# Feed-forwards of an encoder block: a fourth pair by seven products, five sums by DMA, a new head and new ends

## The chip, the cores and the metric

One core of a Trainium2 chip runs one program. The metric is the device time of one execution in microseconds. The engines are TensorE (PE in the profile; PEld is its weight load), VectorE (DVE), ScalarE (ACT), GpSimd (POOL) and SyncE (SP). Transfers between the chip's DRAM and its on-chip memory are issued by SP, ACT or POOL and run on 16 DMA engines.

## The reference, cut to what matters

A layer over 256 tokens of 2048 features: a feed-forward, a mixer of two kinds, attention into 256 memory tokens, a second feed-forward, a last normalisation. All inputs are float32.

```python
def swiglu_ffn(h, w_in, w_out):
    gate, up = jnp.split(h @ w_in, 2, axis=-1)
    return (jax.nn.silu(gate) * up) @ w_out

h = rms_norm(x, ffn1_norm[l])                       # x: (1, 256, 2048)
x = x + 0.5 * swiglu_ffn(h, ffn1_w_in[l], ffn1_w_out[l])   # w_in: (2048, 11264), w_out: (5632, 2048)
...
h = rms_norm(x, ffn2_norm[l])
x = x + 0.5 * swiglu_ffn(h, ffn2_w_in[l], ffn2_w_out[l])
return rms_norm(x, final_norm)
```

## The kernel before, in words

**Two parts for each number.** A float32 operand is split into a high part (a cast to the matmul's float32r format, on ACT) and a low part (the difference, on DVE). A product is three matmuls: high by high, high by low, low by high. `weights` (L112, L113) does this for most matrices; the feed-forwards' input product has `parts` (L339, L340).

**The input product of a feed-forward** is the class `FeedForward`. The 11264 columns are 11 groups of 512 gate and 512 up columns; the 2048 features are 16 k-tiles of 128. A raw weight tile is 128x1024 (512 KB), gate beside up. Group 0 (in `run`) is done k-tile by k-tile while x arrives: `gained` scales x by the norm's gains and splits it, `by_two` does 12 matmuls for a k-tile (lines 288 to 291). Groups 1 to 10 (`group`) take two k-tiles and two token halves together, as 2x2 block products: a pair is done either by eight block products (`eight`, a "C" in the pattern, 24 matmuls) or, in Strassen's way, by seven (`seven`, an "S", 21 matmuls, L275 to L277). The seven need sums of weight blocks (DVE, L388, L389, L394, L401), which are split like weights, and sums of x blocks, made once by `sides`. The pattern of the eight pairs is `SCSCSCCC`. The eight PSUM banks hold b1 to b8; after the last pair by seven a copy and four additions (L439 to L443) take up b1, b5, b6, b7, and at the end of the group four additions (L452) take the others, then `give` makes silu(gate) * up.

**Sums by DMA.** For three k-tiles of a group (`SUMMED`, k = 2, 7, 13, all in pairs by eight) the low part isn't made by DVE: `summed` writes the negated rounded weights to the low part (ACT, L358), the rounded weights to the high part (ACT, L359), and a DMA from POOL's queue reads the raw weights again and adds them to the low part (L360). These tiles have buffers of their own, `hl_s`, and in the first feed-forward also half of `more`. The loads for them go through the same ring of raw tiles as the others.

**Buffers.** Raw tiles: four of the pool `wraw` and five parts of `spare`, in a ring. Split tiles: three of the pool `whl` ("hl"), two of `ring`, and in the first feed-forward one more in `more`, which takes the place of x (`x_given`); x is then read again from its input (L559). In the second feed-forward x stays on chip, so there are two ring tiles and one `hl_s`.

**Order.** Each engine works its instructions in order. The order is made by a scheduler that runs over the traced program with a cost model; `issue_after` puts instructions on an engine behind a given one.

**The head.** SP loads pieces of x transposed, the first parameters, and the raw weights, in that order. The squares of x for the first norm (`x_squares`, L524, L525) load x untransposed into raw tiles of `wraw` at k = 5, 7, 9, 11.

**The end.** The last output product is made for one token half after the other. For each half: the addition to x (`add_up`, L1015), its squares (L1019), and in `give` (L1025 to L1042) the sum over four parts, the root with one correcting step, the scaling and the stores.

## Time and profile before

| | |
|---|---|
| median of 3 runs | 2106.61 us (2106.22 to 2111.86) |
| the profiled execution | 2108.84 us, span 2107.0 us |
| TensorE | 2084.5 us busy, 9764 matmuls |
| VectorE, ScalarE | 1576.8 and 1161.6 us busy |
| DMA | 442.34 MB, 210 GB/s on the mean |
| group 0 to 10 of the first feed-forward | 7 to 474 us |
| the same of the second | about 1390 to 1850 us |

In the rows of the profile `out<-in` names the tiles, x the count, then come the busy time and the mean of one in ns, then the time for which the engine stood idle before them with the releaser. In the rows of stages the columns are the window, its length, the busy time and count of PE, PEld, DVE, ACT and POOL, the granted clock, the share of the 16 DMA engines and GB/s. In a timeline: start, duration, engine, line.

### The profile page before, as it was taken

How to read it: one execution, taken by the hardware profiler on the slowest of the kernel's cores; microseconds unless marked ns; L12 is line 12 of the kernel's file. 1: busy time of each engine (PE TensorE's matmuls, PEld its weight loads, DVE VectorE, ACT ScalarE, POOL GpSimd, SP SyncE). 2: the span in 40 equal slices, each digit the busy share in tenths (PEclk: the TensorE clock that was granted, in tenths of full speed). 3: DMA queues.
4: the chain of work that ended last, by engine and by line, in shares of the span. 5: the costliest groups of instructions: out<-in, count | busy, mean ns of one | idle time of the engine just before them, and what ended most of it. 6: DMA issues, size and time to landing. Idle time of an engine off the chain costs nothing.

```text
span 2107.0 us, 26590 instructions
## 1 busy us (share of the span) xinstructions
PE 2084.5 (99%) x9764; PEld 1738.5 (83%) x9764; DVE 1576.8 (75%) x2215; ACT 1161.6 (55%) x1450; POOL 67.7 (3%) x83
## 2 busy tenths in 40 slices
PE   8999999999999999999999999999999999999998
PEld 6888888888888888888888888888888888888886
DVE  6888888876655589889877665777888887787754
ACT  7666566645544454445665454556665666554443
POOL 0000000000000000000000000000000000000000
PEclk9999999999999999999999999999999999999999
DMA  9778777855666676666565543686787778556664
GB/s 360 230 227 257 229 238 245 263 167 169 216 198 188 206 236 200 190 176 185 176 201 185 186 154 111 206 281 191 231 259 247 232 229 250 178 160 202 197 192 149
DMA packets 122244, 442.34 MB, mean 210 GB/s; under 512 B 13697, under 2 KB 13825, under 8 KB 121729
## 3 DMA queue, kind: packets, MB, share of 16 engines
q1 hardware_dynamic: 113184, 407.35, 58.8%
q0 software_dynamic: 8640, 32.51, 8.5%
q8 instruction: 76, 1.25, 0.2%
q10 hardware_dynamic: 288, 0.79, 0.1%
q14 instruction: 56, 0.45, 0.1%
HBM read 438.49 MB, written 2.10 MB: 209 GB/s over the span
## 4 chain that ended last, share of the span: by engine, by line
PE 84%; issue 11%; DMA 2%; ACT 1%; POOL 1%; DVE 1%; SPq 0%; POOLq 0%; ACTq 0%
PE acc L172 12%; PE acc L173 12%; PE acc L171 12%; PE acc L125 9%; PE acc L289 7%; PE acc L288 7%; PE acc L291 7%; PE acc L126 4%; PE acc L277 2%; PE acc L276 2%; PE acc L275 2%; PE aux L263 1%; PE acc L1066 1%; PE acc L1065 1%; PE acc L1067 1%
## 5 line engine op out<-in xcount | busy, mean ns | idle before, releaser
L113 DVE TENSOR_TENSOR hl<-raw,hl 128x1024 fp32r<-128x1024 f32 (+1 forms) x402 | 488.6, 1216 | 282.5 <-ACT hl L112 281.1
L112 ACT CAST hl<-raw 128x1024 fp32r<-128x1024 f32 (+1 forms) x402 | 419.7, 1045 | 481.6 <-PE acc L173 289.3
L339 ACT CAST hl<-spare 128x1024 fp32r<-128x1024 f32 (+1 forms) x135 | 131.8, 993 | 95.5 <-DVE spare L389 38.5
L340 DVE TENSOR_TENSOR hl<-spare,hl 128x1024 fp32r<-128x1024 f32 (+1 forms) x135 | 154.4, 1150 | 35.8 <-ACT hl L339 34.2
L288 PE MATMUL acc<-hl,x_hl 128*128 128x512 f32 x408 | 144.2, 394 | 9.7 <-ACT hl L339 9.7
L289 PE MATMUL acc<-hl,x_hl 128*128 128x512 f32 x408 | 149.9, 395 | 0.0
L340 DVE TENSOR_TENSOR hl<-raw,hl 128x1024 fp32r<-128x1024 f32 (+1 forms) x101 | 113.9, 1131 | 45.9 <-ACT hl L339 44.3
L339 ACT CAST ring<-spare 128x1024 fp32r<-128x1024 f32 (+1 forms) x99 | 97.2, 988 | 68.9 <-DVE spare L389 26.9
L340 DVE TENSOR_TENSOR ring<-spare,ring 128x1024 fp32r<-128x1024 f32 (+1 forms) x99 | 112.9, 1145 | 19.9 <-ACT ring L339 18.8
L291 PE MATMUL acc<-hl,x_hl 128*128 128x512 f32 x408 | 127.5, 392 | 0.0
L339 ACT CAST hl<-raw 128x1024 fp32r<-128x1024 f32 (+1 forms) x101 | 97.7, 977 | 51.8 <-PE acc L291 16.1
L172 PE MATMUL acc<-hl,x_hl 128*128 128x512 f32 x256 | 100.5, 392 | 0.2 <-DVE hl L113 0.2
L172 PE MATMUL acc<-hl,m_hl 128*128 128x512 f32 x256 | 100.4, 392 | 0.0
L173 PE MATMUL acc<-hl,m_hl 128*128 128x512 f32 x256 | 100.2, 391 | 0.0
L173 PE MATMUL acc<-hl,x_hl 128*128 128x512 f32 x256 | 99.8, 390 | 0.0
L288 PEld LDWEIGHTS acc<-hl,x_hl 128*128 128x128 f32 x408 | 76.8, 189 | 25.9 <-ACT hl L339 10.1
L289 PE MATMUL acc<-ring,x_hl 128*128 128x512 f32 x248 | 93.1, 389 | 0.0
L288 PE MATMUL acc<-ring,x_hl 128*128 128x512 f32 x248 | 91.2, 390 | 0.0
L171 PE MATMUL acc<-hl,m_hl 128*128 128x512 f32 x256 | 91.2, 393 | 0.0
L289 PEld LDWEIGHTS acc<-hl,x_hl 128*128 128x128 f32 x408 | 77.2, 190 | 16.9 <-DVE hl L340 1.1
L291 PEld LDWEIGHTS acc<-hl,x_hl 128*128 128x128 f32 x408 | 77.5, 190 | 16.4
L125 PE MATMUL acc<-x_hl,hl 128*128 128x512 f32 x256 | 91.0, 398 | 0.0
(359 smaller groups left out, 5173.9 us busy)
## 6 DMA issues: line engine op xcount, KB each, us to landing
spare<-in_ffn_w_in SPq DMA_DIRECT2D x192, 512.0 KB, 6.4
raw<-in_ffn_w_out SPq DMA_DIRECT2D x176, 512.0 KB, 3.8
raw<-in_ffn_w_in SPq DMA_DIRECT2D x160, 512.0 KB, 6.3
hl_s<-in_ffn_w_in POOLq DMA_DIRECT2D x44, 512.0 KB, 7.3
raw<-in_w_mix_vg SPq DMA_DIRECT2D x32, 512.0 KB, 4.6
raw<-in_w_k SPq DMA_DIRECT2D x32, 512.0 KB, 4.0
raw<-in_w_v SPq DMA_DIRECT2D x32, 512.0 KB, 4.4
raw<-in_w_mix_out SPq DMA_DIRECT2D x32, 512.0 KB, 4.6
```

The costliest lines, as they stand in the source:

```text
L112: nc.scalar.copy(out=hl[:, 0, :size], in_=raw[:, :size])
L113: newest[0] = nc.vector.tensor_tensor(out=hl[:, 1, :size], in0=raw[:, :size], in1=hl[:, 0, :size].bitcast(F32), op=ALU.subtract)
L125: nc.tensor.matmul(acc, lhsT=w_hi, rhs=x_hl, start=first, stop=False, skip_group_check=True)
L126: nc.tensor.matmul(acc[:, 0], lhsT=w_lo, rhs=x_hl[:, 0], start=False, stop=last, skip_group_check=True)
L171: nc.tensor.matmul(acc[t], lhsT=x[:, 0, s], rhs=hi[:, k], start=k0 + k == 0, stop=False)
L172: nc.tensor.matmul(acc[t], lhsT=x[:, 0, s], rhs=lo[:, k], start=False, stop=False)
L173: nc.tensor.matmul(acc[t], lhsT=x[:, 1, s], rhs=hi[:, k], start=False, stop=k0 + k == nk - 1)
L288: nc.tensor.matmul(acc[t][g], lhsT=x[:, 0, s], rhs=hi[:, cols[g]], start=(t, g) in first, stop=False)
L289: nc.tensor.matmul(acc[t][g], lhsT=x[:, 0, s], rhs=lo[:, cols[g]], start=False, stop=False)
L291: nc.tensor.matmul(acc[t][g], lhsT=x[:, 1, s], rhs=hi[:, cols[g]], start=False, stop=last)
L339: nc.scalar.copy(out=hl[:, 0, :n], in_=raw[:, :n])
L340: newest[0] = nc.vector.tensor_tensor(out=hl[:, 1, :n], in0=raw[:, :n], in1=hl[:, 0, :n].bitcast(F32), op=ALU.subtract)
```

## The change

- Pattern `SCSCSCSC` in both feed-forwards: four of the eight pairs by seven products. `sides` makes a fourth set of x sums at k = 15 of group 0.
- Five k-tiles of a group (2, 6, 7, 11, 14) are summed by DMA. Their raw loads have one, later two, raw tiles of their own, taken from the ring, which goes from nine to eight, later seven.
- ACT's work for the next summed tile is put behind the cast of the k-tile that follows.
- The second feed-forward also gets the third ring tile and the second tile for sums: x is stored to DRAM behind the attention (`kept`, four stores) and read again after the last group (`x_back`).
- Head: the gains and the first k-tile of x come as one array by ACT's queue, the first weight tile in two halves; 11 plain float32 matmuls of `ones` stand ahead of the first product (`WARM`); the squares of x use tiles of `h` and come at k = 2, 4, 6, 8; the other parameters come at k = 6.
- Group 0's `give` stands ahead of `x_given` and of the second `summed`.
- In the last group two instead of four of the transposes that follow are done beside the last pairs.
- The end: three of the four sums of squares are added ahead of the last part; the fourth is added as the bias of the root; one operation changes its form.

```diff
-PATTERNS = ("SCSCSCCC", "SCSCSCCC")
-SUMMED = ((2, 7, 13), (2, 7, 13))
+PATTERNS = ("SCSCSCSC", "SCSCSCSC")
+SUMMED = ((2, 6, 7, 11, 14), (2, 6, 7, 11, 14))
+WARM = 11
...
+    gx = xt.tile([P, KD + KD * T], F32, name="gx", tag="x")
+    gains, xT = gx[:, :KD], gx[:, KD:].rearrange("p (k t) -> p k t", t=T)
+    nc.scalar.dma_start(out=gx[:, :KD + T], in_=a["gains_x0"])
+    nc.scalar.dma_start(out=xT[:, 1], in_=a["xT"][:, 1])
+    nc.vector.memset(ones, 1.0)
+    idle = pa.tile([P, 2, T], F32, name="aux")
+    for _ in range(WARM):
+        nc.tensor.matmul(idle[:, 0, :P], lhsT=ones, rhs=ones, start=True, stop=True)
...
+    def x_given():
+        more = xt.tile([P, 4, 1024], F32R, name="more", tag="x")
+        ff.ring.append(more[:, :2])
+        ff.hls.append(more[:, 2:])
+        ff.raws_summed.append(ff.raws.pop())
+    def x_back(src):
+        xT = xt.tile([P, KD, T], F32, name="xT", tag="x")
+        for k in range(0, KD, 8):
+            nc.gpsimd.dma_start(out=xT[:, k:k + 8], in_=src[:, k:k + 8])
+        return xT
...
     (FeedForward.__init__)
+            self.raws_summed = [self.raws.pop()]
     (summed)
-            raw, hl = self.raw(j, k), self.hls[at % len(self.hls)]
+            raw, hl = self.raws_summed[at % len(self.hls)], self.hls[at % len(self.hls)]
+            nc.sync.dma_start(out=raw, in_=self.w_in[j, :, k])
     (end of seven)
+            if self.next is not None:
+                with tc.issue_after(self.cast.ins):
+                    self.summed(self.next)
+                self.next = None
     (eight)
-                if at is not False:
-                    self.summed(at + len(self.hls))
+                if self.next is not None:
+                    with tc.issue_after(self.cast.ins):
+                        self.summed(self.next)
+                self.next = None if at is False else at + len(self.hls)
     (group)
-                    if p > self.spairs[-1] + 1:
+                    if p >= n - 2:
...
+        def early(self, before):
+            self.raw_at += 1
+            self.at += 1
+            raw = wraw.tile([P, 1024], F32, name="raw")
+            hl = whl.tile([P, 2, 1024], F32R, name="hl")
+            halves = [slice(G, 2 * G), slice(0, G)]
+            for s in halves:
+                nc.sync.dma_start(out=raw[:, s], in_=self.w_in[0, :, 0, s])
+            x = before(0)
+            for s in halves:
+                with tc.issue_after(x.ins):
+                    split(hl[:, 0, s], hl[:, 1, s], raw[:, s])
+            return hl
     (run)
+            self.give(0, [acc[t][0] for t in range(2)], [acc[t][1] for t in range(2)], r)
             if more is not None:
                 more()
                 self.summed(1)
-            self.give(0, [acc[t][0] for t in range(2)], [acc[t][1] for t in range(2)], r)
...
-                    now, turns = turns[:4], turns[4:]
+                    at = 2 * self.pattern[-2:].count("C")
+                    now, turns = turns[:at], turns[at:]
...
     (x_squares)
-        raw = wraw.tile([P, 1024], F32, name="raw")
+        raw = ff.h[7 - c].rearrange("p a b -> p (a b)")
     (x_arrives)
-            if k % 2 == 0:
+            if k > 0 and k % 2 == 0:
                 nc.sync.dma_start(out=xT[:, k:k + 2], in_=a["xT"][:, k:k + 2])
-            if k == 0:
-                nc.sync.dma_start(out=pv[:, :head], in_=a["pv"][:, :head])
     (x_more)
-            if k in (5, 7, 9, 11):
-                x_squares(k // 2 - 2)
-            if k in (6, 9, 12):
+            if k in (2, 4, 6, 8):
+                x_squares(k // 2 - 1)
+            if k in (6, 9, 12, 15):
                 ff.sides(k // 3 - 2)
...
     (the output product of the attention)
+                if f % 4 == 3:
+                    nc.gpsimd.dma_start(out=kept[:, f - 3:f + 1], in_=xT[:, f - 3:f + 1])
...
-        turns = ff.run(lambda k: None, first_beside, lambda: rms_cols(ss, D, "r_x2"))
+        turns = ff.run(lambda k: None, first_beside, lambda: rms_cols(ss, D, "r_x2"), x_given)
+        xT = x_back(kept)
...
     (the end)
-            nc.vector.reduce_sum(out=tot, in_=sums[:, t], axis=AX.X)
-            nc.scalar.activation(out=s, in_=tot, func=AF.Sqrt, scale=1.0 / D, bias=eps)
-            nc.vector.tensor_scalar(out=v, in0=tot, scalar1=1.0 / D, scalar2=RMS_EPS, op0=ALU.mult, op1=ALU.add)
+            last = sums[:, t, 3:4]
+            nc.scalar.activation(out=s, in_=last, func=AF.Sqrt, scale=1.0 / D, bias=most[t])
+            nc.vector.tensor_scalar(out=v, in0=last, scalar1=1.0 / D, scalar2=most[t], op0=ALU.mult, op1=ALU.add)
             nc.vector.reciprocal(out=r, in_=s)
-            nc.vector.scalar_tensor_tensor(out=r, in0=v, scalar=r, in1=s, op0=ALU.mult, op1=ALU.add)
+            nc.vector.tensor_scalar(out=r, in0=v, scalar1=r, scalar2=s, op0=ALU.mult, op1=ALU.add)
```

More of the change, by code (lines that the diff above doesn't have):

```diff
@@ L237, in gained @@
     def gained(dst, k, x, g):
-        nc.scalar.activation(out=dst[:, k, 0], in_=x, func=AF.Copy, scale=g)
+        part = nc.scalar.activation(out=dst[:, k, 0], in_=x, func=AF.Copy, scale=g)
         nc.vector.scalar_tensor_tensor(
@@ L242, in gained @@
         )
+        return part
     def gained_tile(tag):
@@ L338, in parts @@
             hl = whl.tile([P, 2, 1024], F32R, name="hl") if last or i < 3 else self.ring[i - 3]
-            nc.scalar.copy(out=hl[:, 0, :n], in_=raw[:, :n])
+            self.cast = nc.scalar.copy(out=hl[:, 0, :n], in_=raw[:, :n])
             newest[0] = nc.vector.tensor_tensor(
@@ L367, in sides @@
             for q in range(2):
-                nc.scalar.activation(out=xg[:, q], in_=xT[:, k + q], func=AF.Copy, scale=col(self.gain, k + q))
+                nc.scalar.activation(out=xg[:, q], in_=xT[:, k + q], func=AF.Copy, scale=self.gain(k + q))
             a11, a21, a12, a22 = xg[:, 0, :P], xg[:, 0, P:], xg[:, 1, :P], xg[:, 1, P:]
@@ L453, in group, with run @@
             self.give(j, (p1, u2), (u4, u5), r)
-        def run(self, before, after, root, more=None):
+        def early(self, before):
[11 more added lines that the diff above has]
+            return hl
+        def run(self, before, after, root, more=None, early=False):
             acc = token_accs()
@@ L459, in run @@
             for k in range(KD):
-                before(k)
-                w = self.parts(self.raw(0, k))
+                if k == 0 and early:
+                    w = self.early(before)
+                else:
+                    before(k)
+                    w = self.parts(self.raw(0, k))
                 begin = [(t, g) for t in range(2) for g in range(2)] if k == 0 else []
@@ L548, in x_root @@
             return r_x
-        def x_given():
-            more = xt.tile([P, 4, 1024], F32R, name="more", tag="x")
-            ff.ring.append(more[:, :2])
-            ff.hls.append(more[:, 2:])
-        turns = ff.run(x_arrives, x_more, x_root, x_given)
-        xT = xt.tile([P, KD, T], F32, name="xT", tag="x")
-        for k in range(0, KD, 8):
-            nc.gpsimd.dma_start(out=xT[:, k:k + 8], in_=a["xT"][:, k:k + 8])
+        turns = ff.run(x_arrives, x_more, x_root, x_given, early=True)
+        xT = x_back(a["xT"])
         sm = st.tile([P, T], F32, name="sm")
@@ L1022, in give @@
         def give(t, parts):
[L1024 to L1027 removed]
+            v, s, r = [st.tile([P, 1], F32, name=f"{n}{t}") for n in ("f_v", "f_s", "f_r")]
+            last = sums[:, t, 3:4]
+            nc.scalar.activation(out=s, in_=last, func=AF.Sqrt, scale=1.0 / D, bias=most[t])
+            nc.vector.tensor_scalar(out=v, in0=last, scalar1=1.0 / D, scalar2=most[t], op0=ALU.mult, op1=ALU.add)
             nc.vector.reciprocal(out=r, in_=s)
[L1029 removed]
+            nc.vector.tensor_scalar(out=r, in0=v, scalar1=r, scalar2=s, op0=ALU.mult, op1=ALU.add)
             nc.vector.reciprocal(out=r, in_=r)
@@ L1050, in layer @@
         finish()
+        st.tile([P, 8], F32, name="to_64_too")
+        most = [st.tile([P, 1], F32, name=f"f_most{t}") for t in range(2)]
+        for t in range(2):
+            nc.vector.reduce_sum(out=most[t], in_=sums[:, t, 0:3], axis=AX.X)
+            nc.vector.tensor_scalar(
+                out=most[t], in0=most[t], scalar1=1.0 / D, scalar2=RMS_EPS, op0=ALU.mult, op1=ALU.add
+            )
         warm = nc.scalar.activation(out=st.tile([P, 1], F32, name="warm"), in_=ones[:, 0:1], func=AF.Sqrt)
```

25 lines of the change are left out of this document (11 added, 14 removed).

## The prediction

> **What bounds the kernel now.** I read the page first (busy time, slices, DMA queues), then the busy time by stage, then the order of time inside a feed-forward group. From the page:
>
> ```profile
> span 2107.0 us, 26590 instructions
> ...
> PE 2084.5 (99%) x9764; PEld 1738.5 (83%) x9764; DVE 1576.8 (75%) x2215; ACT 1161.6 (55%) x1450; POOL 67.7 (3%) x83
> ...
> q1 hardware_dynamic: 113184, 407.35, 58.8%
> q0 software_dynamic: 8640, 32.51, 8.5%
> ```
>
> TensorE is busy 99% of the span. A busy TensorE can still wait inside its pipeline, so the next question is the spacing of the starts. Two rows of the timeline of TensorE within a group of the first feed-forward; the first and the last of 49 consecutive starts, with 48 matmuls of 128x512 from one to the other:
>
> ```profile
> 329.66 0.39 PE L275 MATMUL acc<-ring,x_hl 128*128 128x512 f32 x1
> ...
> 340.54 0.39 PE L288 MATMUL acc<-hl_s,x_hl 128*128 128x512 f32 x1
> ```
>
> 10.88 / 48 = 0.2267 us for one matmul, without a gap. The stages (columns: length, then busy time and count of PE, PEld, DVE, ACT, POOL, then granted clock, DMA share, GB/s):
>
> ```profile
> 0.00:7.10 7.10, 0.00 (x0) 0.00 (x0) 2.15 (x9) 4.68 (x10) 0.70 (x6) 1.00 0.72 220
> 7.10:41.85 34.75, 34.74 (x143) 28.36 (x144) 25.77 (x39) 29.02 (x44) 1.88 (x2) 1.00 1.03 386
> 41.85:58.00 16.15, 13.57 (x53) 10.44 (x52) 8.46 (x15) 8.54 (x10) 0.00 (x0) 0.89 0.80 289
> 58.00:473.50 415.50, 415.03 (x1836) 343.25 (x1835) 339.99 (x406) 250.34 (x278) 24.62 (x29) 1.00 0.74 233
> ...
> 1435.00:1850.00 415.00, 414.03 (x1830) 341.99 (x1829) 335.64 (x403) 251.18 (x275) 24.38 (x28) 1.00 0.76 230
> ...
> 2097.00:2107.00 10.00, 0.03 (x1) 0.00 (x0) 4.02 (x11) 3.29 (x7) 1.26 (x1) 0.67 0.55 211
> ```
>
> 1830 matmuls at 0.2267 are 414.9 us: the ten groups of the second feed-forward (415.00) are nothing but matmuls, and those of the first (415.5) nearly so. A matmul left out there is worth its 0.2267 us, as long as the other engines and the DMA keep up. Beside this stand three places where TensorE does not run: 7.1 us at the start, the head (143 matmuls take 34.75 us where 32.4 would do; 53 take 16.15 where 12.0 would do), and 10 us at the end.
>
> **The change, part by part.**
>
> *Matmuls.* A pair by seven products is 7 x 3 = 21 matmuls, by eight 24. One more pair by seven in each of ten groups of both feed-forwards: 20 x 3 = 60 matmuls fewer, 60 x 0.2267 = 13.6 us. Group 0 keeps its 192.
>
> *DVE and ACT per group.* Their prices, by form, from the steady part of the first feed-forward:
>
> ```profile
> L340 DVE TENSOR_TENSOR hl<-spare,hl 128x1024 fp32r<-128x1024 f32 x38 | 46.1, 1221 | 6.0 <-ACT hl L339 5.7
> ...
> L388 DVE TENSOR_TENSOR spare<-raw 128x512 f32<-128x512 f32 x12 | 8.2, 687 | 5.2 <-DMA raw<-in_ffn_w_in 5.2
> ...
> L340 DVE TENSOR_TENSOR hl<-raw,hl 128x512 fp32r<-128x512 f32 x7 | 4.8, 690 | 3.4 <-ACT hl L339 3.1
> ...
> L339 ACT CAST hl<-spare 128x1024 fp32r<-128x1024 f32 x39 | 40.5, 1050 | 27.2 <-DVE spare L389 18.5 <-PE acc L277 4.1 <-DMA spare<-in_ffn_w_in 2.7
> ...
> L339 ACT CAST hl<-raw 128x512 fp32r<-128x512 f32 x7 | 4.3, 619 | 5.1 <-DVE raw L401 5.1
> ```
>
> and the same stretch and one of the second feed-forward as a whole (eight and seven groups):
>
> ```profile
> 100.00:432.00 332.00, 332.00 (x1466) 274.99 (x1466) 275.17 (x329) 203.56 (x226) 20.90 (x24) 1.00 0.77 242
> 1518.00:1808.00 290.00, 289.28 (x1276) 239.27 (x1275) 239.37 (x287) 179.63 (x196) 18.33 (x21) 1.00 0.79 240
> ```
>
> A seven costs DVE four half operations (0.69), three whole ones (1.22) and a half one (0.69): 7.1 us; a k-tile in the plain way 1.22. Of the k-tiles in eights, 7 were plain; now 3 of 8 are (five are summed by DMA). So DVE changes by +7.1 - 4 x 1.22 = +2.2 us: from 275.17/8 = 34.4 to 36.6 us, in a group that shrinks from 41.5 to 40.8 us: 83% to 90%. ACT: +3.8 (three casts of 1.05 and one of 0.62) - 4 x 1.05 + 2 summed tiles at two operations of about 1.05 = +3.8: 25.4 to 29.2 us, 72%. Both stay under the matmuls; this I cost at nothing where work is spread, and what covers it is the lead of three tiles "hl" and now three of the ring in both feed-forwards. The lead is real now: ACT waited for TensorE (rows below).
>
> *DMA.* Each summed tile is read twice. From the queue rows an accumulating transfer (0.524 MB; 62 of them in q0's 32.51 MB) takes 8.5% x 2107 / 62 = 2.9 us of all 16 engines. Two more per group: the share goes from 0.77 x 41.5 = 32.0 to 37.8 of 40.8 us, 0.92 (second feed-forward 0.94), at (16 + 5) x 0.524 MB / 40.8 us = 270 GB/s. The head sustained a share of 1.03 and 386 GB/s while TensorE ran, so the transfers fit; they land later. Seven raw tiles for 11 loads that remain in the ring, beside two of the summed tiles' own, replace nine for 16: 26 us of holding time against 23, so I cost the smaller ring at nothing.
>
> *The summed chain.* After TensorE's last reading of a summed tile come ACT's negated copy, POOL's issue, the landing, and TensorE's next use. One such chain of the second feed-forward, from k=2 to k=7, and the landings of all:
>
> ```profile
> 1687.11 0.61 PE L291 MATMUL acc<-hl_s,x_hl 128*128 128x512 f32 x2
> ...
> 1687.31 1.07 ACT L358 ACTIVATE hl_s<-spare 128x1024 fp32r<-128x1024 f32 x1 [1.17 <-PE acc L289]
> ...
> 1688.78 0.87 POOL L360 DMA_DIRECT2D hl_s<-in_ffn_w_in  x1 [12.04 <-ACT hl_s L358]
> ...
> 1698.22 0.39 PE L288 MATMUL acc<-hl_s,x_hl 128*128 128x512 f32 x1
> ```
>
> ```profile
> DMA to landing us min/median/max: 5.3/7.3/9.8
> ```
>
> The chain is 1.67 us and a landing; 11.1 us are there (45 matmuls and the end of a tile). With two tiles a summed k-tile uses the buffer of the one two before it: 2 to 7 and 6 to 11 have this distance, 7 to 14, 11 to the next 2 and 14 to the next 6 have 15 us or more. So 40 tight chains in all, with a margin of 2.1 us at the median landing, none at 9.4. In the old first feed-forward every distance was longer, in the second one two of three were as tight, and cost
>
> ```profile
> PE acc L289 <- DMA hl_s<-in_ffn_w_in: 1.0, 2, 0.7
> ```
>
> 1.0 us in all at a DMA share of 0.79. Bounds for the new one: 0 (none late) and 40 x 0.8 = 32 us (each landing as late as 9.8 or a little more, where the scheduler leaves less than 11.1). I take 2.5 us, near the measured 1.0, for twice the tight chains of which some land later. The new place of the casts changes the order on ACT: the copy now stands behind the next k-tile's cast, which runs ahead of TensorE, so it is not held up; nothing is gained on the path either. At group ends the last seven is now followed by one pair of eight (5.4 us) instead of three (16.3): four DVE additions and a copy, some 3.4 us, must free the banks in it. They fit; I add 1 us in all for this and for bursts (0 to 8 by 20 ends at 0.4).
>
> *Head.* Rows of the first 45 us:
>
> ```profile
> 0.84 0.17 DVE L186 MEMSET ones<- 128x128 f32 x1 [0.84 <-PEq L1135]
> ...
> 7.11 2.07 PE L288 MATMUL acc<-hl,x_hl 128*128 128x512 f32 x4 [7.11 <-ACT hl L339]
> ...
> 42.69 1.06 ACT L525 ACTIVATE raw<-raw 128x1024 f32<-128x1024 f32 x1 [1.92 <-DMA raw<-in_x]
> ```
>
> ```profile
> 874.72 0.60 PE L774 MATMUL aux<-wT,vs 128*128 128x128 f32 x4
> ```
>
> The first matmuls come 0.43 us apart (four in 2.07 us), twice the later spacing. The filler is 11 matmuls of plain f32; the last row is two such (four passes, about 0.11 each at the full clock), so one costs 0.22, or 0.44 at the slow start: 11 x 0.44 = 4.8 us from about 1.1, to 5.9 us. The data are there by then: smaller loads, with no wait for the parameters. So the real start moves from 7.1 to 5.9 (-1.2), and of the 2.3 us lost to slow matmuls I take 1.6 back (bounds 0 and 2.3). The 4.1 us lost after 41.85 began with ACT waiting for a late piece of x (row L525), which had waited for a raw tile; x's squares now have tiles of their own and come three k-tiles sooner, so this wait goes. What is late next is the weights: the DMA was full from 7 to 42 us (1.03), the bytes are the same and TensorE comes 3 us sooner. I take half: -2.1 (bounds 0 and -4.1).
>
> The Trainium skill (TensorE: Matmul & The Clock Gate, section "What's actually happening") has a free-running window of 3413 ns after which the clock is released; the slow start here is in keeping with it. By that rule a filler begun at 1.1 us releases the clock between about 4.5 and 7.9 us, and this term would lie between -2.3 and -1.3, so the sum would move by less than a microsecond.
>
> *Ends.* Rows of the first token half's end:
>
> ```profile
> 2095.60 0.16 DVE L1025 TENSOR_REDUCE f_tot<-sums 128x1 f32<-128x4 f32 x1 [0.79 <-ACT sq L1019]
> 2095.64 1.30 POOL L1020 TENSOR_TENSOR spare<-spare,gf 128x512 f32<-128x512 f32 x1 [53.70 <-ACT sq L1019]
> 2095.79 0.15 DVE L1027 TENSOR_SCALAR f_v<-f_tot 128x1 f32<-128x1 f32 x1
> ...
> 2096.32 0.64 DVE L1029 SCALAR_TENSOR_TENSOR f_r<-f_v,f_r,f_s 128x1 f32<-128x1 f32 x1
> ```
>
> The reduction leaves the chain (0.19) and the form of 0.64 becomes one of 0.15: -0.68 in each half. The first half's chain keeps DVE from the second's addition, so both count: -1.3 us.
>
> *x in DRAM.* Four stores of 512 KB and a load of 2 MB, on POOL's queue, under matmuls; the load is wanted about 3 us after the last group and can start when the third ring tile is done, before the last pair. Nothing, at worst 4 us once. Two transposes fewer ahead of the output product: the same.
>
> **Sum.** -13.6 - 1.2 - 1.6 - 2.1 - 1.3 + 2.5 + 1.0 = -16.3 us. The profiled execution took 2108.84 us (span 2107.0), so it would take 2092.5; the median of the three runs stands 2.2 us below it, and so my time is 2090 us.
>
> **The rivals.**
>
> *A. Late accumulates (slower).* If the landing under a share of 0.92 to 0.94 passes 9.4 us as a rule, TensorE waits twice a group. At 0.8 us it is 32 us instead of 2.5: 2090 + 29.5 = 2120. It outweighs the gains of 19.8 us from 0.5 us a chain. For it: landings up to 9.8 already. Against it: at 0.79 TensorE lost only the 1.0 us above, and the head moved 386 GB/s. The Trainium skill (SBUF — State Buffer, "Who interferes with whom" and the warning above it) says that descriptors for POOL's transfers wait while DVE holds a shared port, which would feed this rival; it also says that an addition with two SBUF inputs blocks only reads, and that fits POOL's even 0.87 us here.
>
> *B. DVE and ACT become the bound.* These rows of the waits, over all 20 groups:
>
> ```profile
> DVE hl L340 <- ACT hl L339: 78.5, 76, 5.1
> ...
> DVE ring L340 <- ACT ring L339: 33.3, 38, 2.9
> ...
> ACT hl_s L358 <- PE acc L289: 31.8, 30, 3.7
> ...
> ACT hl L339 <- PE acc L291: 25.6, 23, 1.9
> ```
>
> DVE waits 112/20 = 5.6 us a group for casts. Were this forced by the order (sum, cast, difference), DVE would need 36.6 + 5.6 = 42.2 us against 40.8, 1.4 x 20 = 28 us, 2118; with half of it forced, 39.4, no loss. In between, 41.7 gives +18, 2108: no change. Against: ACT itself waits for TensorE, so much of the idle time is lead.
>
> *C. The head stays as it was.* The DMA is full there whatever is asked for: without -4.9 us, 2095.
>
> *D. Everything goes well.* No stall, the whole head: -13.6 - 1.2 - 2.3 - 4.1 - 1.3 = -22.5: 2084.
>
> **Chances.** My case with C and D as its edges (2083 to 2098): 0.70. A mild form of A or B with still a gain (2098 to 2100): 0.07; about no change (2100 to 2113): 0.09; clearly slower: 0.14. What a measurement can tell from no change is some 0.3%, 6.3 us. So faster 0.77, same 0.09, slower 0.14. The range reaches from 2082 to 2106, the likeliest case's own from 2083 to 2098.
>
> **What would show it.** Right: 22 records of filler and 60 matmuls fewer than before, groups of 40.8 us with DVE at 0.90 and the DMA share at 0.92; first matmul on weights near 5.9 us and no gap near 42; waits of TensorE for the two summed tiles of a few microseconds in all; no 0.6 us operation in the end. Wrong: groups over 41.2 us; TensorE waiting for L340 or L339 (B) or for the accumulates (A); ACT or DVE waiting for raw tiles for more than now. The prediction fails if landings grow beyond 9.4 us, or if the tight chain starts later on ACT than 0.2 us after TensorE's last reading.

## The result and the profile after

| | median | range |
|---|---|---|
| before | 2106.61 us | 2106.0 to 2111.86, 5 runs |
| after | 2128.6 us | 2125.21 to 2132.5, 5 runs |

The ratio is 1.0101 (95% interval 1.0089 to 1.0112): the change made the kernel 1% slower. The prediction was 2090.

The page of the kernel after (span, busy times, and POOL's DMA queue with the accumulating transfers):

```profile
span 2123.4 us, 26702 instructions
...
PE 2093.7 (99%) x9726; PEld 1730.7 (82%) x9726; DVE 1614.3 (76%) x2307; ACT 1221.7 (58%) x1537; POOL 104.7 (5%) x129
...
q0 software_dynamic: 15264, 57.68, 13.9%
```

TensorE has fewer matmuls (9726 records for 9764: 60 fewer, and 22 of the filler) and is busy 9 us longer. A busy share of 99% says nothing here; the stages do. First before, cut at starts of matmuls (start, group 0, groups 1 to 10, the stretch from the first output product on, and so on; the groups end with the start of their last matmul; columns as in the prediction):

```profile
0.00:7.11 7.11, 0.00 (x1) 0.00 (x1) 2.16 (x9) 4.69 (x10) 0.70 (x6) 1.00 0.72 220
7.11:57.53 50.42, 47.84 (x193) 38.40 (x193) 33.74 (x53) 37.08 (x54) 1.88 (x2) 0.97 0.96 358
57.53:474.48 416.95, 416.48 (x1843) 344.42 (x1842) 341.44 (x408) 250.81 (x278) 24.62 (x29) 1.00 0.74 233
474.48:1386.46 911.98, 910.57 (x4562) 769.21 (x4561) 659.72 (x1038) 475.65 (x668) 1.18 (x9) 1.00 0.61 187
...
1430.46:1847.75 417.29, 416.32 (x1838) 343.91 (x1837) 337.48 (x403) 253.27 (x278) 24.38 (x28) 1.00 0.76 230
1847.75:2096.64 248.89, 248.89 (x1137) 206.07 (x1136) 165.30 (x249) 109.47 (x125) 12.53 (x7) 1.00 0.61 180
2096.64:2107.00 10.36, 0.39 (x2) 0.00 (x0) 4.35 (x12) 3.29 (x7) 1.56 (x2) 0.68 0.53 203
```

The same stages after:

```profile
0.00:5.77 5.77, 4.71 (x23) 4.71 (x23) 1.06 (x3) 3.15 (x8) 0.70 (x6) 1.00 0.68 225
5.77:50.96 45.19, 44.51 (x194) 36.23 (x194) 37.66 (x66) 38.63 (x60) 1.03 (x1) 1.00 1.03 392
50.96:472.69 421.73, 414.80 (x1801) 336.35 (x1800) 355.01 (x443) 281.79 (x317) 42.92 (x50) 1.00 0.86 254
472.69:1393.43 920.74, 917.35 (x4575) 771.67 (x4573) 662.67 (x1041) 476.91 (x671) 2.78 (x12) 1.00 0.61 188
...
1437.41:1854.84 417.43, 413.34 (x1800) 336.62 (x1799) 354.94 (x442) 279.97 (x314) 41.98 (x49) 1.00 0.86 254
1854.84:2113.88 259.04, 254.66 (x1146) 208.58 (x1144) 168.05 (x258) 108.53 (x128) 11.53 (x7) 0.99 0.59 178
2113.88:2123.40 9.52, 0.39 (x2) 0.00 (x0) 3.53 (x9) 3.20 (x7) 1.48 (x2) 0.78 0.57 221
```

The head gained 6.6 us (1.34 and 5.23), the end 0.84. The groups should have gained 13.6 us and lost instead: +4.8 in the first feed-forward and +0.1 in the second. And two stages that the prediction left alone lost 18.9: the stretch that begins with the first output product +8.8, the second output product +10.2. Together this is +16.4 us, the difference of the spans.

What makes these up is read from the starts of consecutive matmuls of 128x512. What a step has above 0.2267 us is an excess; in a step under 0.30 us it is counted as slow spacing, in a longer one as a wait or as a matmul at half the clock (0.43 us):

| us against before | matmuls | waits and half clock | slow spacing | transposes moved out of the groups, and other shapes |
|---|---|---|---|---|
| groups, both feed-forwards | -13.6 | +13.7 | +6.6 | -1.8 |
| after them, both output products | 0 | +9.6 | +5.1 | +4.1 |

The 4.1 us hold the two waits for ACT of 0.8 us each that stand behind transposes. TensorE's waits after (what was waited for: us in all, times, longest):

```profile
PE acc L303 <- DMA more<-in_ffn_w_in: 7.5, 9, 2.0
PE acc L176 <- DVE hl_s L124: 5.2, 2, 3.6
PE acc L289 <- DVE spare L489: 1.9, 4, 0.8
PE acc L174 <- ACT hl_s L123: 1.6, 2, 0.8
...
PE aux L289 <- DVE spare L479: 0.8, 1, 0.8
PE acc L303 <- DMA hl_s<-in_ffn_w_in: 0.7, 1, 0.7
```

So there are three suspects: the groups, with tiles summed by DMA that come late (first and last row) and waits for DVE's evictions (third and fifth); the start of the output products (second and fourth); and a spacing of matmuls that no wait explains. Each was taken apart on the chip. The kernel before was timed again beside each set of runs (medians 2107.1 to 2108.6 us); the ratios below are taken against those runs.

### The profile page after: what moved, and what is told of

The parts are those of the page before. It is cut to its first block, busy times and chain, and to the rows that moved or that the text cites. A ratio compares the mean times of both kernels' runs of the same rounds, so it can differ in the third digit from the quotient of the medians.

```text
span 2123.4 us, 26702 instructions
## 1 busy us (share of the span) xinstructions
PE 2093.7 (99%) x9726; PEld 1730.7 (82%) x9726; DVE 1614.3 (76%) x2307; ACT 1221.7 (58%) x1537; POOL 104.7 (5%) x129
## 3 DMA queue, kind: packets, MB, share of 16 engines
q10 hardware_dynamic: 576, 1.06, 0.1%
## 4 chain that ended last, share of the span: by engine, by line
PE 67%; issue 26%; DMA 3%; POOL 3%; ACT 1%; DVE 1%; SPq 0%; POOLq 0%; DVEq 0%; ACTq 0%
PE acc L176 12%; PE acc L175 12%; PE acc L174 12%; PE acc L128 8%; PE acc L129 4%; PE acc L303 3%; PE acc L305 2%; PE acc L302 2%; DMA more<-in_ffn_w_in 2%; POOL hl_s L391 1%; POOL more L391 1%; PE aux L277 1%; PE acc L291 1%; PE acc L290 1%; PE acc L289 1%
## 5 line engine op out<-in xcount | busy, mean ns | idle before, releaser
L116 DVE TENSOR_TENSOR hl<-raw,hl 128x1024 fp32r<-128x1024 f32 (+1 forms) x402 | 488.7, 1217 | 290.4 <-ACT hl L115 289.4
L370 DVE TENSOR_TENSOR hl<-spare,hl 128x1024 fp32r<-128x1024 f32 (+1 forms) x102 | 116.7, 1146 | 12.0 <-ACT hl L369 11.7
L369 ACT CAST hl<-spare 128x1024 fp32r<-128x1024 f32 (+1 forms) x102 | 100.1, 989 | 38.2 <-DVE spare L432 16.0
L369 ACT CAST hl<-raw 128x1024 fp32r<-128x1024 f32 (+1 forms) x109 | 101.8, 944 | 33.7 <-DVE raw L432 25.2
L369 ACT CAST ring<-spare 128x1024 fp32r<-128x1024 f32 (+1 forms) x84 | 82.2, 988 | 54.4 <-PE acc L291 27.4
L370 DVE TENSOR_TENSOR ring<-spare,ring 128x1024 fp32r<-128x1024 f32 (+1 forms) x84 | 95.4, 1143 | 19.0 <-ACT ring L369 18.7
L175 PE MATMUL acc<-hl,x_hl 128*128 128x512 f32 x256 | 100.5, 393 | 0.0
L176 PE MATMUL acc<-hl,x_hl 128*128 128x512 f32 x256 | 99.9, 390 | 0.0
L303 PE MATMUL acc<-more,x_hl 128*128 128x512 f32 x240 | 89.2, 394 | 7.5 <-DMA more<-in_ffn_w_in 7.5
L128 PE MATMUL acc<-o_hl,hl 128*128 128x512 f32 x256 | 90.6, 399 | 0.0
L128 PE MATMUL acc<-y_hl,hl 128*128 128x512 f32 x256 | 90.5, 399 | 0.0
L174 PE MATMUL acc<-hl,x_hl 128*128 128x512 f32 x256 | 90.0, 391 | 0.0
L175 PE MATMUL acc<-hl,hA 128*128 128x512 f32 x224 | 87.9, 392 | 0.0
L175 PE MATMUL acc<-hl,hB 128*128 128x512 f32 x224 | 87.4, 390 | 0.0
L302 PE MATMUL acc<-more,x_hl 128*128 128x512 f32 x240 | 86.8, 390 | 0.0
L176 PE MATMUL acc<-hl,hA 128*128 128x512 f32 x224 | 84.8, 390 | 0.0
```

Of the source, the lines that this page charges most:

```text
L116: newest[0] = nc.vector.tensor_tensor(out=hl[:, 1, :size], in0=raw[:, :size], in1=hl[:, 0, :size].bitcast(F32), op=ALU.subtract)
L128: nc.tensor.matmul(acc, lhsT=w_hi, rhs=x_hl, start=first, stop=False, skip_group_check=True)
L174: nc.tensor.matmul(acc[t], lhsT=x[:, 0, s], rhs=hi[:, k], start=k0 + k == 0, stop=False)
L175: nc.tensor.matmul(acc[t], lhsT=x[:, 0, s], rhs=lo[:, k], start=False, stop=False)
L176: nc.tensor.matmul(acc[t], lhsT=x[:, 1, s], rhs=hi[:, k], start=False, stop=k0 + k == nk - 1)
L302: nc.tensor.matmul(acc[t][g], lhsT=x[:, 0, s], rhs=hi[:, cols[g]], start=(t, g) in first, stop=False)
```

## The experiments

### Slow spacing: where the operands lie

The slow matmuls are those whose operand is `hl_s` or `hC`. One output tile's 48 consecutive matmuls on `hC`, first and last start, before:

```profile
593.28 0.62 PE L171 MATMUL acc<-hl,hC 128*128 128x512 f32 x2
...
603.93 0.39 PE L173 MATMUL acc<-hl,hC 128*128 128x512 f32 x1
```

and after:

```profile
598.28 0.63 PE L174 MATMUL acc<-hl,hC 128*128 128x512 f32 x2
...
609.25 0.39 PE L176 MATMUL acc<-hl,hC 128*128 128x512 f32 x1
```

10.65 / 47 = 0.2266 us a matmul against 10.97 / 47 = 0.2334, at a granted clock of 1.00 in both and with no wait. What changed is the place: the 16 gains (64 bytes in each partition) left the tile `pv` and now lie ahead of x in `gx`. The tiles between the two moved down by 64 bytes, while `hl_s` and `hC`, behind x, stayed. Modulo 256 bytes all these tiles started at 64 before; now `hl`, `x_hl`, the ring and `more` start at 0, `hl_s` and `hC` still at 64. So it is not the place of one tile: `hC` at 64 is fast beside `hl` at 64, and `hl` at 0 is fast beside `x_hl` at 0.

**64 bytes put into the kernel before.**

```diff
     xT = xt.tile([P, KD, T], F32, name="xT", tag="x")
+    xt.tile([P, 16], F32, name="shift", tag="shift")
```

> The kernel before with 64 bytes of padding ahead of hl_s and hC and nothing else. If the place of the operands sets the spacing, matmuls with hl_s or hC go from 0.2267 to 0.232 to 0.234 us: 176 x 3 matmuls in the groups with hl_s and some 650 with hC and hl_s in the output products, 1170 x 0.006 = 7 us more, 2113. If it doesn't, the time stays at 2106.6 and the spacing at 0.227.

Measured: 2113.67 us (2112.58 to 2116.3), ratio 1.0039 (1.0024 to 1.0054); 48 matmuls on `hC` again take 10.97 us from the first start to the last. Sixteen unused floats cost 6.3 us against the median of 2107.33 of the kernel before on the same chip (5 to 11 us by the interval of the ratio).

**64 bytes more in the kernel after**, which makes the offset 128.

```diff
-    gx = xt.tile([P, KD + KD * T], F32, name="gx", tag="x")
+    gx = xt.tile([P, KD + KD * T + 16], F32, name="gx", tag="x")
...
```

> The changed kernel with the tile that holds x made 64 bytes longer, so that hl_s and hC (and all that lies behind them) move by 64 bytes; the other operands of TensorE stay, and the order of the instructions is the same. In the changed kernel x_hl, hl, ring and more begin at a multiple of 128 bytes, hl_s and hC 64 bytes off one (before, all of them were 64 off), and matmuls that pair hl_s or hC with another tile start 0.232 to 0.234 us apart instead of 0.2267. Theory (operands of TensorE that differ by 64 bytes modulo 128 read slower together): all matmuls of the two feed-forwards and the output products are back at 0.227; the slow spacing costs 6.6 us in the groups and some 5 us in the stages behind them, so 8 to 12 us less, some 2117 to 2121. Rival (something else reads or writes beside them, the extra accumulating DMAs first): hl_s and hC stay at 0.232 to 0.234, time within 2 us of the changed kernel's 2128.6.

Measured: 2127.37 us (2124.39 to 2132.52), the spacing on `hC` 0.2324. The offset of 128 bytes is nearly as slow as 64, so the idea that 128 would be enough fell.

**256 bytes in the kernel before** (one run): `xt.tile([P, 64], ...)` in the place of 16.

> The kernel before with 256 bytes of padding ahead of hl_s and hC, to see which distance matters. If operands must agree modulo 512 bytes or more, the spacing of matmuls with hl_s and hC is 0.231 to 0.234 us as with 64 bytes, and the time near 2113; if modulo 256 or less, 0.227 and 2107.

```profile
1963.40 0.61 PE L171 MATMUL acc<-hl,hC 128*128 128x512 f32 x2
...
1974.05 0.39 PE L173 MATMUL acc<-hl,hC 128*128 128x512 f32 x1
```

10.65 us again, and 2106.02 us in all. The offsets tried are 0 and 256 (fast), 64 and 128 (slow).

**The kernel after with the operands placed as before**: the gains get a tile of their own ahead of the others.

```diff
+    gains = const.tile([P, KD], F32, name="gains")
-    gx = xt.tile([P, KD + KD * T], F32, name="gx", tag="x")
-    gains, xT = gx[:, :KD], gx[:, KD:].rearrange("p (k t) -> p k t", t=T)
+    xT = xt.tile([P, KD, T], F32, name="xT", tag="x")
...
```

> The changed kernel with the 16 gains of a partition in a tile of their own ahead of the large buffers, in place of the first 64 bytes of the tile that holds x; gains and first k-tile of x come by two transfers. Every operand of TensorE is then where it was before the change, and hl, ring, more, x_hl, hl_s and hC begin at the same residue modulo 4096 bytes. Theory now (the spacing is 0.2267 only where the two operands of matmul and weight load begin at the same residue modulo a larger power of two than 128; a shift by 64 or by 128 bytes breaks it): hl_s and hC go from 0.232 to 0.234 back to 0.227, 6 us come back in the groups and some 5 behind them: 2116 to 2120. Rival (the extra accumulates or the order slow these reads): spacing and time stay, 2126 to 2130.

Measured: 2120.99 us (2116.12 to 2123.28), ratio 1.0060 (1.0039 to 1.0081), 7.6 us under the change. The spacing is back: 48 matmuls on `hC` take 10.66 us from the first start to the last. The 7.6 us are less than was expected and less than the 11.7 that the steps gave to the spacing (6.6 + 5.1): in the profiled executions the groups' waits rose from 16.7 to 19.2 us, which takes a part of it; where the rest went stays open.

### The start of the output products

An eviction is an addition on DVE that takes a bank of PSUM up. DVE at the end of the second feed-forward, after (a timeline: the evictions L477 to L480 and L489, weights' low parts L116, transposes of x L1037, the gate L457, and only then the low part of the turned, that is transposed, h, L124):

```profile
1850.58 0.69 DVE L480 TENSOR_TENSOR spare<-spare,acc 128x512 f32<-128x512 f32 x1
...
1860.30 0.61 DVE L1037 STREAM_TRANSPOSE spare<-xT 32x128 f32<-32x128 f32 x2
1860.93 1.29 DVE L124 TENSOR_TENSOR hl_s<-aux,hl_s 128x512 fp32r<-128x512 f32 x2
```

and TensorE, which needs it:

```profile
1857.70 0.39 PE L175 MATMUL acc<-hl,hl_s 128*128 128x512 f32 x1
1861.68 1.22 PE L176 MATMUL acc<-hl,hl_s 128*128 128x512 f32 x2 [3.58 <-DVE hl_s L124]
```

Before, this L124 (there L121) ran ahead of the group's end, which was at 1847.75:

```profile
1844.91 1.29 DVE L121 TENSOR_TENSOR hl_s<-aux,hl_s 128x512 fp32r<-128x512 f32 x2
```

With each of the two long waits the granted clock goes down; what follows at the first output product (first row) and at the second:

```profile
477.59:481.00 3.41, 3.41 (x8) 2.67 (x9) 1.21 (x2) 0.00 (x0) 0.00 (x0) 0.52 0.53 154
...
1861.68:1868.50 6.82, 6.82 (x22) 5.48 (x23) 3.03 (x5) 1.53 (x2) 0.00 (x0) 0.63 0.19 68
```

At the first output product the longest wait was 1.64 us, and the next 3.4 us passed at a granted clock of 0.52. The Trainium skill (TensorE: Matmul & The Clock Gate, "What's actually happening") has the half clock after an idle window of some 3.4 us; the length of this slow stretch agrees, but here two shorter waits, of 0.79 and 1.64 us with four matmuls between them, were enough.

**Four transposes beside the last pair** instead of two.

```diff
                     if p >= n - 2:
-                        for _ in range(2):
+                        for _ in range(4):
...
-                    at = 2 * self.pattern[-2:].count("C")
+                    at = 4 * self.pattern[-2:].count("C")
```

> The changed kernel with four instead of two transposes of h done beside the last pair of the last group, as many as before the change. Theory (two transposes are too short a lead: TensorE waits for the first split tiles of h at the start of both output products and falls back to half its clock): the waits there go, 1.0 + 1.8 + 0.4 and eight times 0.2 us in the first, 1.0 + 3.8 + 0.4 and nine times 0.2 in the second, so 8 to 12 us less, 2117 to 2121. Rival (the wait comes from the order on DVE and ACT, which are late with the last group's gate): a gain under 3 us, or the last group gets longer by as much.

Measured: 2130.43 us (2129.04 to 2132.68), ratio 1.0118 (1.0102 to 1.0133). The waits for `hl_s` stay:

```profile
PE aux L277 <- DVE hl_s L124: 5.2, 2, 3.6
...
PE acc L174 <- ACT hl_s L123: 1.6, 2, 0.8
```

The first now stands at the transposes (L277). The number of transposes taken ahead isn't the cause.

**The last group alone in the old order `SCSCSCCC`**, so that three pairs by eight stand behind the last evictions.

> The changed kernel with the last group of each feed-forward in the old pattern (three pairs by seven, two by eight at the end, four transposes beside them); the nine other groups as changed. It has 6 matmuls more (1.4 us). Theory (with a pair by seven just ahead of the last pair the evictions, the gate and the transposes' splits all fall on DVE in the last 5.4 us, and TensorE waits 5.2 + 1.6 us for hl_s and runs some 3 to 6 us at half its clock): these waits go, 8 to 12 us less at both ends together, 1.4 us more for the matmuls: 2118 to 2122. Rival (the output product's start is slow for another reason): the waits for hl_s stay and the time is 2129 to 2131.

Measured: 2121.49 us (2116.05 to 2123.56), ratio 1.0061 (1.0039 to 1.0084). No wait for `hl_s` is left at either output product, and the second one takes 250.99 us instead of 259.03. What was missing is time between the last pair by seven and the end of the group: with one pair by eight there, the evictions and what is queued behind them filled DVE just when it should have split the turned h.

### The groups

**The old pattern and its three sums in the new kernel.**

```diff
-PATTERNS = ("SCSCSCSC", "SCSCSCSC")
-SUMMED = ((2, 6, 7, 11, 14), (2, 6, 7, 11, 14))
+PATTERNS = ("SCSCSCCC", "SCSCSCCC")
+SUMMED = ((2, 7, 13), (2, 7, 13))
...
```

> The changed kernel with the old pattern (three of eight pairs by seven products) and the old three sums by DMA in both feed-forwards; head, ends, filler, x in DRAM and the raw tiles as changed. Theory (the fourth pair by seven with its five sums costs waits in the groups that eat its 13.6 us): the groups are back at 41.5 us without waits, their 60 matmuls cost 13.6 us again, the head's 6.6 and the end's 0.8 us stay gained, the slow spacing of hl_s and hC stays in part, and four transposes stand beside the last two pairs again: 2100 to 2108. Rival (the rest of the change is what costs): over 2112.

Measured: 2106.44 us (2104.57 to 2107.45), ratio 0.9997 (0.9987 to 1.0007). The reported waits in the groups are gone, the head's gain stays, and the slow spacing takes that gain back. With the operands placed as before as well:

> The three-of-eight pattern of before with its three sums, and from the change the head, the second x in DRAM, the separate raw tiles, the later accumulates, the lent buffers in the second feed-forward and the ends; the operands placed as before. If the placement's cost adds to the rest, the 2106.4 of the same kernel without the placement falls by about 7.5 (slow spacing 3.8 in the feed-forwards, 5 in the output products, of which about 1.5 stays): 2099 (range 2096 to 2102), spacing of the matmuls on hl_s and hC 0.227. If not (something else holds the three-of-eight groups at their time): 2103 to 2106.

Measured: 2099.32 us (2098.59 to 2100.3), ratio 0.9957 (0.9944 to 0.9971). The head, the ends and the lent buffers together are worth 8 us once the placement is right.

**Three tiles for sums and two of the ring**, instead of two and three.

> The changed kernel with three tiles for sums by DMA and two in the ring, in place of two and three: a summed k-tile uses the buffer of the one three before it, so the shortest distance goes from 45 matmuls (10.2 us) to 66 (15 us); the load on the DMA is the same. Theory (late accumulates: too short a distance): TensorE's waits for more and hl_s go from 8.2 us (9 in this manner of order) to under 1 us, and some of that comes back in time: 2118 to 2124. Rival (the DMA as such is the limit): waits for accumulates or for raw tiles stay at 8 us or more, 2127 or above. Second rival (the smaller ring takes the lead of ACT and DVE): waits of TensorE for L369 or L370 appear in their place.

Measured: 2153.39 us (2149.7 to 2158.1), ratio 1.0211 (1.0189 to 1.0232). The waits for the sums stay (6.4 us for `more`, 2.1 for `hl_s`), which was not expected; the waits for the evictions grow (`spare` L489: 10.0 us for 1.9), and new ones for split tiles appear: the ring's third tile is needed more than a third buffer for sums.

**Placement and last group together, five sums as in the change.**

> The changed kernel with both repairs that worked apart: the operands placed as before, and the last group in the old order of pairs. Five tiles are summed as in the change. If the two costs are independent, the time is that of the placed kernel (2121.0) less what the last group's order took away there (out2's wait 7.8 to 1.8, and about as much at the first output product's turned tiles, 2): 2113 (range 2109 to 2117), with about 20 us of waits still in the groups, most of them for more, hl_s and spare. If the waits in the groups only move with the faster matmuls (a tile that comes late stays late however fast TensorE is), they grow by what the placement gains there and the time stays at 2118 to 2122.

Measured: 2111.93 us (2108.35 to 2114.03), ratio 1.0017 (1.0008 to 1.0026): the two costs add, as the first theory said. What is left are the groups' waits:

```profile
PE acc L305 <- DMA more<-in_ffn_w_in: 9.1, 7, 2.6
PE aux L291 <- DVE spare L483: 4.9, 6, 1.4
PE acc L291 <- DVE spare L493: 1.2, 3, 0.8
```

**Four sums (2, 6, 10, 14)**, else the same.

> The changed kernel with the operands placed as before (gains in a tile of their own), the old order of pairs in the last group, and four tiles summed by DMA in each group (2, 6, 10 and 14) instead of five, so that two sums in one buffer stand 17.7 us apart instead of 10.2 to 11.4. Theory A (the accumulates' turn-round in two buffers makes the waits inside the groups): no wait for hl_s or more is left in the groups, the groups' waits fall from about 22 us (14.8 and 7.6 in the run with the last group alone) to under 6, and the time is about 2098 (range 2094 to 2104). Theory B (VectorE, at 0.9 of the span and with one more subtraction of about 1.1 us in each group, is the bound of four-of-eight groups): the waits go over to the parts, to spare (the running sums) and to the evictions, together 15 us or more, and the time is 2110 to 2120.

Measured: 2100.64 us (2097.18 to 2102.69), ratio 0.9963 (0.9949 to 0.9977):

```profile
PE acc L291 <- DVE spare L493: 3.0, 5, 1.5
PE acc L305 <- DMA hl_s<-in_ffn_w_in: 2.2, 3, 0.9
PE aux L291 <- DVE spare L483: 2.2, 3, 1.0
```

A sum fewer, and 11 us less, although DVE has a subtraction more in each group. By the steps between matmuls the groups' waits went from 25.2 to 13.5 us. Neither theory fits whole: A has the time right, but 2.2 us of waits for a sum and 5.2 for evictions (`spare`) are left.

**One raw tile for the sums** in the kernel with four sums, so that the weights' ring has eight again.

```diff
-        ff.raws_summed.append(ff.raws.pop())
-            raw, hl = self.raws_summed[at % len(self.hls)], self.hls[at % len(self.hls)]
+            raw, hl = self.raws_summed[0], self.hls[at % len(self.hls)]
```

> The four-sums kernel (operands placed as before, last group in the old order, sums at 2, 6, 10, 14), with one raw tile for both sum buffers, so that the second one stays in the ring of the weights (eight instead of seven). If the smaller raw ring makes the 13.5 us of waits in the groups (sums wait 25.6 us for raw tiles on VectorE): half of it or more goes, 2092 to 2096. If the ring isn't what is late (VectorE's evictions and sums are): within 1.5 us of 2100.6. If the one raw tile delays the sums: hl_s is waited for longer than 2.2 us and the time is above 2102.

Measured: 2150.95 us (2149.28 to 2155.22), ratio 1.0207 (1.0192 to 1.0222). The waits moved to another place than the third case named:

```profile
PE acc L291 <- ACT more L370: 19.8, 5, 5.9
PE acc L291 <- ACT hl L370: 15.9, 5, 3.8
```

The timelines of SP's queue and of ACT show it at one such place:

```profile
220.92 11.90 SPq L389 DMA_DIRECT2D spare<-in_ffn_w_in  x2
...
230.48 1.06 ACT L390 ACTIVATE more<-spare 128x1024 fp32r<-128x1024 f32 x1 [5.31 <-DMA spare<-in_ffn_w_in]
...
232.38 1.04 ACT L370 CAST more<-spare 128x1024 fp32r<-128x1024 f32 x1
```

The second load of a sum can't be issued before ACT has read the first one out of the only tile, and SP issues no weight load behind it for the 11.9 us between them; ACT stands still for the load, with the cast behind it that TensorE waits for. The sums need their second raw tile far more than the ring needs its eighth.

**The order `SCSSCSCC`** in all groups, the last one too, sums at 2, 8, 12, 14, the operands placed as before.

```diff
-PATTERNS = ("SCSCSCSC", "SCSCSCSC")
-SUMMED = ((2, 6, 7, 11, 14), (2, 6, 7, 11, 14))
+PATTERNS = ("SCSSCSCC", "SCSSCSCC")
+SUMMED = ((2, 8, 12, 14), (2, 8, 12, 14))
...
```

> Operands placed as before; every group in the order SCSSCSCC (four pairs of seven and two pairs of eight behind the last of them, in the last group too), sums at 2, 8, 12, 14. 60 matmuls fewer than the old order, as in the change. If the evictions with one pair behind them make the remaining waits: no wait of the group's first seven-product matmul for spare, groups' waits below 5 us in all, 2088 to 2092. If VectorE's load is the bound, the two adjoining pairs of seven make a new wait in the middle of the group for their sums (spare, the added operands) of about 1 us a group: 2098 to 2106.

Measured: **2089.57 us** (2087.03 to 2093.32), ratio 0.9919 (0.9902 to 0.9935), faster than both kernels. TensorE's waits in the feed-forwards' groups and the groups as a whole:

```profile
PE acc L304 <- DMA more<-in_ffn_w_in: 2.3, 3, 1.8
```

```profile
50.28:462.13 411.85, 409.57 (x1809) 338.26 (x1807) 366.67 (x455) 274.14 (x309) 34.20 (x40) 1.00 0.84 251
...
1417.95:1827.10 409.15, 408.99 (x1808) 338.48 (x1807) 366.63 (x456) 272.35 (x306) 33.29 (x39) 1.00 0.83 250
```

1800 matmuls at 0.2267 are 408.1 us: the second feed-forward stands at 1 us above it, with DVE busy 366.63 / 409.15 = 90%. So VectorE's load was not the bound. Against the kernel with four sums the waits for evictions went from 5.2 us to none, while those for sums stayed (2.2 and 2.3 us): this speaks for the order, with two pairs by eight behind the last pair by seven instead of one. But the positions of the sums changed with it, and which of the two took how much stays open.

**The same order with one raw tile for the sums.**

> The order SCSSCSCC with sums at 2, 8, 12, 14, the operands placed as before, and one raw tile for the sums, so that the ring has eight. If ring and order each take a part of the 13.5 us: 2087 to 2091, under both of the other two. If only the order counts, as that kernel alone; if VectorE's load is the bound, 2098 to 2106 as well.

Measured: 2137.94 us (2134.43 to 2142.25), ratio 1.0143 (1.0126 to 1.0160): the cost of sharing the raw tile again, 48 us here and 50 there.

The medians, step by step: 2128.6 (the change), 2121.0 (placement), 2111.9 (last group), 2100.6 (four sums), 2089.6 (order). They were taken beside different timings of the kernel before, which differ by 2 us.

## Why the prediction was wrong

Three steps failed: a cost that had no term (the operands' place), a cover taken as given (at the end of the last group at nothing, at the groups' ends and bursts at 1.0 us), and a margin that was mis-sized (the summed chain). Between the profiled execution (2125.21 us) and the 2092.5 of the sum lie 32.7 us. By the table of steps the spacing has 11.7 of them, the waits in the groups 10.2 (13.7 where 2.5 + 1.0 were predicted), the start of the output products 9.6, and the transposes and other shapes 2.3 (4.1 - 1.8). The head gave 1.7 more than its 4.9, the ends 0.5 less than their 1.3. Together that is 32.6.

- *Matmuls.* Right: 60 fewer. The 13.6 us appear only where little else is late: the last kernel is 9.7 us under the one with the old pattern (2099.3), and its groups still wait 3.7 us. That its 2089.6 comes so near the predicted 2090 is luck in part: it has another order and a sum fewer, and its terms are not those of the sum.
- *Operands' place.* No term of the sum. The change moves 64 bytes, which the diff shows, and the prediction took 0.2267 as fixed for every matmul of the shape. Measured: 11.7 us in the spacing, 7.6 by the repaired kernel's median.
- *"Two transposes fewer ahead of the output product: the same"*, that is, nothing, at worst 4 us. It is not their number (four cost as much as two); the cover failed. The transposes' splits stood behind DVE's evictions, and the prediction's paragraph on group ends had put these into one pair by eight (5.4 us) with the words "They fit". It counted the additions, some 3.4 us, and not what stands behind them in DVE's queue at the last group. It cost 9.6 us of waits and half clock.
- *The summed chain.* The mechanism was named (rival A), and it struck where the prediction looked for it: the ten reported waits for an accumulate, 8.2 us where 2.5 were predicted, beside the restarts, all stand in the 40 chains that it called tight, two of the twenty from k = 2 to 7 and eight of the twenty from 6 to 11. What was mis-sized is the margin of 2.1 us. The quoted chain began and ended at other matmuls than those that read the low part. From the last reading of the low part to the next one the trace has 10.05 us from 2 to 7 and 11.46 from 6 to 11 (medians, waits included), not 11.1 each. POOL's issue came 1.9 us after the last reading in the first and 2.43 in the second, where the sum had 1.67, and the landings took 7.0 and 8.4 us, though the DMA share was 0.86 and not 0.92. In twelve of the twenty chains from 6 to 11 less than 0.1 us lay between the landing and the matmul that needed it. Of the two signs that the prediction named last, landings over 9.4 us came mostly where they do no harm (13 of 15 in the chain from 7 to 14); the late start of ACT's copy came true: 0.97 us after the last reading for k = 11 against 0.43 for k = 7 (medians, from start to start). One late case, from the timelines of the engines:

```profile
407.86 0.39 PE L303 MATMUL acc<-more,x_hl 128*128 128x512 f32 x1
...
407.00 1.57 ACT L369 CAST hl<-spare 128x512 fp32r<-128x512 f32 x2 [3.87 <-DVE spare L432]
...
409.43 1.05 ACT L369 CAST hl<-spare 128x1024 fp32r<-128x1024 f32 x1
410.38 1.05 ACT L389 ACTIVATE more<-spare 128x1024 fp32r<-128x1024 f32 x1
...
411.83 0.86 POOL L391 DMA_DIRECT2D more<-in_ffn_w_in  x1 [10.79 <-ACT more L389]
...
421.15 0.73 PE L303 MATMUL acc<-more,x_hl 128*128 128x512 f32 x2 [1.97 <-DMA more<-in_ffn_w_in]
```

  ACT had waited 3.87 us for one of DVE's sums, so its casts stood ahead of the copy, which came 2.5 us after TensorE's last reading; the transfer then took 9.3 us, and TensorE waited for the last 2 of them. Here a late sum on DVE was paid at the accumulate.
- *Bursts and group ends.* 1.0 us predicted; 2.7 of waits for `spare` in the change, 6.1 in the kernel with placement and last group repaired. The new order brought 11 us (1.4 of them the six matmuls fewer in the two last groups).
- *Rival B* (DVE and ACT as the bound) fell as a matter of load: 90% busy and no wait for DVE in the groups of the last kernel. DVE's time a group was 35.5 us in the change (355.01 / 10) where 36.6 were predicted, and 36.7 in the last kernel, which has one DMA sum fewer.
- *The smaller raw ring* at nothing: not tested alone, but the second feed-forward of the last kernel has it and stands 1 us above its matmuls. Giving the tile back at the sums' cost lost 50 us. x in DRAM: no wait for it was seen.
- *Head.* Better than said: 6.6 instead of 4.9. The filler ran from 1.06 us, and the first matmul on weights came at 5.77 (5.9 said). The wait after 42 us is nearly gone, where only half of it had been taken.
- *Ends.* 0.84 measured for 1.3. The new form on DVE (L1075), priced at 0.15 us, took 0.27.

## What to carry to other kernels

When an engine at 99% gets less work, ask at every place where it could wait not how busy the helper is but what the helper has queued at that moment. Additions that must follow a burst need a stretch of plain work behind them. A tile that one engine frees and another queue waits for blocks all that stands behind it in that queue. Treat the time of one matmul as something to measure for each pair of tiles, and after any change of a tile's size look at where the tiles behind it start.

## What the runs showed of the hardware

The spacing of matmuls (128x128 by 128x512, float32r, at a granted clock of 1.00) depends on where their two operands start against each other: 0.2267 us when the starts agree modulo 256 bytes (offset 0 and 256), 0.2334 at an offset of 64 and 0.2324 at 128, 2.5 to 3% more. The Trainium skill (TensorE: Matmul & The Clock Gate, "Step-by-step: what each phase is for") has two independent read ports on TensorE, so that loading weights takes nothing from the running matmul. A spacing that changes with the two starts together does not agree with that for these shapes; by what means the offset acts, none of the runs shows.
